# Prompt and sample step of an mLSTM–HGRN2 layer: another order of projection blocks, keys and queries in one tile, and weight sums that a transfer adds in place

## The chip, the cores and the metric

The kernel runs on one core of a Trainium2 chip. The metric is the device time of one execution in microseconds (us). Before the change the median of three runs is 1180.33 us (1180.24 to 1180.45).

The engines are named as in the profile: PE (matrix multiply, with its weight loads as PEld), DVE (vector), ACT (scalar), POOL (GpSimd), SP (which issues most transfers). Each engine works through its own list of instructions in order and waits at one instruction until the semaphores of that instruction are there; what stands behind it waits too.

## The reference

One step of a hybrid layer over 544 tokens: 512 of a new prompt and 32 of a running stream. All matrices are float32.

```python
xn = rmsnorm(x); proj = xn @ w_in                       # 1024 -> 12 blocks of columns
u, v, z, ig, fg, q_h, f_h, i_h, g_h, ga, gb = split(proj)
c  = silu(causal_conv(u))
hm = mlstm(c @ w_qm, c @ w_km, v, ig, lf, C, n, m)      # 4 heads of 512, chunks, matrix memory C
hm = (layernorm(hm) + m_skip * c) * silu(z);  ya = hm @ w_brm
f  = lb + (1 - lb) * sigmoid(f_h);  k = (1 - lb) * sigmoid(-f_h);  q = silu(q_h)
oh = hgrn(q, k, i_h, log f, S)                          # 8 heads of 128, gated linear attention
oh = head_rmsnorm(oh) * silu(g_h);               yb = oh @ w_brh
h  = x + (sigmoid(ga) * ya + sigmoid(gb) * yb) @ w_out
h  = h + sigmoid(h @ w_pg) * (p @ w_ple);        out = rmsnorm(h)
```

The new states (convolution rows, C, n, m, S) of both streams are outputs as well.

## The kernel before

**Numbers.** Every float32 product is made of three: an operand is split into a high part (ACT rounds it, L103 or L130) and the rest (DVE subtracts, L104 or L131), and PE multiplies high by high, high by low and low by high.

**Projections.** The product of `xn` with the columns of `w_in` goes by *units* of 128 output columns, two units a and b at a time (a *pair*, class `Two`). The inner dimension of 1024 is cut in half, so the weights of a pair are four pieces of 128x512: a11 and a12 (unit a, first and second half), a21 and a22 (unit b). A Strassen-like scheme makes seven products instead of eight, with a11, a12, a22 and the sums s1 = a21 + a22, s2 = s1 + a11, s3 = a11 + a21, s4 = s2 + a12. Each of the seven is a *block*: a 128x512 piece, cast by ACT and completed by DVE, then 4 x 3 matmuls of 272 columns into one of the pair's two PSUM halves (tile `d`). Between blocks ACT copies a partial result out (`keep`, L481, tile `t`), and DVE adds or subtracts a partial result into the destination (`put`, L488 and L490). a11, s2, s3 and a22 gather in the first half, a12, s1 and s4 in the second. The sums s1 and s3 of *early* pairs are not computed by DVE: SP loads one piece into a tile `ws` (L404) and POOL issues a second transfer that adds the other (L405). s2 and s4 are added by DVE (L430). So POOL holds such a transfer until the load of its base has landed.

**Order.** PE's list is written out by hand (`manual_schedule`); the lists of DVE, ACT, POOL and SP follow the program order and priorities through a scheduler. `Pump` holds all blocks of all pairs of a stage, sorted by times from a table (`HEAD` for a first pair, `NEXT` for the others: the blocks of one pair interleave with those of the next), and emits them in half steps of six matmuls. *Chains* (`mchain` for a head of the mLSTM, `chain` for a head of HGRN2) yield numbers; at each yield that many half steps of projection go onto PE's list, and the weights of up to `AHEAD` = 3 blocks more are prepared. Rings of buffers bind this: raw pieces `NRAW` = 8, high and low pieces `NPIECE` = 5 each, sums `NSUM` = 5, token-wide tiles `NSLOT` = 26.

**Stages.** After the norm come four mLSTM heads: projections run beside the chain of the head; at its end the head's result `hm` (four tiles, L1083 to L1085 and the split at L104) is multiplied by `w_brm` in `stage_br` (24 matmuls for each of eight results, tile `ya`, weights `wbm..`), and for heads after the first DVE adds the former sum (`y`, L1103). For the last head, 16 half steps of the HGRN2 projections are pumped ahead of `stage_br(3)`. Then the eight HGRN2 heads: for each, the pairs q/f and g/i, and `chain(h)`. It has seven levels c = 1, 2, 4, ..., 64: ACT packs keys into `km` (L1438), three half steps of projection follow, four matmuls give `pl` (L1446), DVE scales half of the keys and half of the queries (`hk`, `hq`, L1464, in four operations) and copies the level's part of `pl` under a mask into `at` (L1473). After the last level keys are transposed (`ht`, L1510), the output `ho` is formed, and ACT scales the head's output by the root-mean-square factor `hr` (L1564, four 128x128 pieces, and L1565). Then come eight pairs `ga` and `gb` (the merge), `p @ w_ple`, `yb`, `w_out` and `w_pg`.

The order of a pair's blocks, and what the pump does before the last `stage_br`:

```python
ALONE, HEAD, NEXT = (0, 1, 2, 3), (0, 3, 1, 6, 5, 9, 11), (0, 3, 5, 6, 8, 9, 11)   # a11 s2 a12 s3 s1 a22 s4
...
pump.to(8 * LASTBR)
stage_br(MH - 1)
```

## Time and profile before

| what | value |
|---|---|
| median of three runs | 1180.33 us |
| the profiled execution, its own time | 1178.68 us |
| its span in the trace | 1176.7 us |
| PE busy | 1140.0 us, 8897 records |
| DVE busy | 891.7 us (76%) |
| ACT busy | 708.9 us (60%) |
| POOL busy | 181.6 us (15%) |
| mean granted clock of PE | 0.997 |

The span lies 1.98 us below the execution's own time. Stages by the trace: head 0's `ya` runs at 179.1 to 203.6 us, the last head's `ya` at 619.0 to 651.3, the HGRN2 heads between about 650 and 950, the merge after that. A row of the windows view gives, for a stretch from A to B, its length, then busy time and count for PE, PEld, DVE, ACT and POOL, the granted clock of PE, the share of time that the transfer engines were busy, and GB/s. A row of the waits view gives the instruction that waited, the one that released it, the sum in us, how often, and the longest.

### The profile page before, as it was taken

The page shows a single profiled execution, that of the slowest core. Times are in us where ns is not written, and L with a number is a line of the kernel's source. Part 1 is how long each engine was busy: PE and PEld are TensorE (multiplying, and loading weights), DVE is VectorE, ACT ScalarE, POOL GpSimd, SP SyncE. Part 2 cuts the span into 40 slices and gives each one's busy share as a digit, 9 for nine tenths or more (in the row PEclk, how much of TensorE's full clock was granted, in tenths as well). Part 3 has the DMA queues.
Part 4 walks back from the last instruction along what each step waited for, and adds up shares of the span by engine and source line. Part 5 has one row for each costly group of instructions (what it writes and reads, how often), then busy time and mean ns, then how long its engine had stood idle before and what let it go on. Part 6 is the DMA issues. An engine that isn't in the chain of part 4 may idle for free. (4 is left out here: it accounts for less than half of the span.)

```text
span 1176.7 us, 24263 instructions
## 1 busy us (share of the span) xinstructions
PE 1140.0 (97%) x8897; PEld 1110.7 (94%) x8897; DVE 891.7 (76%) x2092; ACT 708.9 (60%) x1565; POOL 181.6 (15%) x335
## 2 busy tenths in 40 slices
PE   9999999999999999999988999999999989999998
PEld 9998999999999999999977999899989989999998
DVE  6977987686996768967883788898888767654485
ACT  5676567554765547565552577777777755433462
POOL 4942001110011001110100112221122210000000
PEclk9999999999999999999989999999999999999999
DMA  6233215232452324434836544544444585332653
GB/s 228 64 117 103 93 48 183 100 110 99 137 175 92 107 102 130 158 121 144 243 94 209 137 123 113 117 108 111 118 116 125 142 236 150 110 98 78 235 169 113
DMA packets 88270, 154.69 MB, mean 131 GB/s; under 512 B 9940, under 2 KB 17492, under 8 KB 88152
## 3 DMA queue, kind: packets, MB, share of 16 engines
q1 hardware_dynamic: 81072, 140.50, 36.5%
q0 software_dynamic: 6912, 12.59, 6.9%
q8 instruction: 70, 1.15, 0.4%
q14 instruction: 48, 0.39, 0.1%
q10 hardware_dynamic: 168, 0.06, 0.0%
HBM read 128.19 MB, written 24.91 MB: 130 GB/s over the span
## 5 line engine op out<-in xcount | busy, mean ns | idle before, releaser
L405 POOL DMA_DIRECT2D ws<-in_w_in x48 | 42.1, 877 | 301.8 <-DMA ws<-in_w_in 57.4
L481 ACT COPY t<-d 128x272 f32<-128x272 f32 x126 | 47.5, 377 | 2.7 <-PE d L467 2.2
L1446 PE MATMUL pl<-hq,km 128*128 128x128 f32 x224 | 37.1, 289 | 8.6 <-ACT km L1438 8.5
L601 DVE SCALAR_TENSOR_TENSOR cv<-ub,vec,cv 128x547 f32<-128x547 f32 x48 | 40.3, 841 | 2.9 <-ACT cv L596 2.1
L1446 PEld LDWEIGHTS pl<-hq,km 128*128 128x128 f32 x224 | 30.9, 190 | 11.0 <-ACT km L1438 10.8
L965 DVE SCALAR_TENSOR_TENSOR c<-c,wi,Cs 128x258 f32<-128x258 f32 x32 | 15.3, 478 | 21.6 <-PE Cs L963 21.5
L1438 ACT COPY km<-hk 128x256 f32<-128x256 f32 x56 | 23.5, 419 | 10.3 <-DVE rsq_u L168 5.8
L1103 DVE TENSOR_TENSOR y<-ya,y 128x272 f32<-128x272 f32 x48 | 18.8, 434 | 13.6 <-PE ya L151 13.4
L877 ACT COPY Co<-C 128x258 f32<-128x258 f32 x32 | 10.4, 378 | 28.9 <-PE C L865 22.1
L1473 DVE COPY_PREDICATED at<-lmask,pl 128x288 f32<-128x288 uint8 (+1 forms) x56 | 26.3, 469 | 0.0
L1464 DVE TENSOR_TENSOR hq<-hq,q 128x128 f32<-128x128 f32 (+1 forms) x96 | 25.2, 290 | 0.9
L1421 POOL TENSOR_SCALAR_AFFINE_SELECT aa<-at 128x128 f32<-128x128 f32 x32 | 25.5, 829 | 2.3 <-DVE at L1473 2.3
L1464 DVE TENSOR_TENSOR hk<-hk,q 128x144 f32<-128x144 f32 (+1 forms) x96 | 25.1, 290 | 0.7
L593 POOL COPY uo<-ub 128x3 f32<-128x3 f32 x16 | 17.5, 1092 | 39.0 <-DVE ub L490 28.8
L1046 ACT COPY y<-nm 128x516 f32<-128x516 f32 x16 | 9.4, 590 | 21.6 <-PE nm L1035 21.6
L763 POOL COPY vsm<-vt 128x96 f32<-128x96 f32 x16 | 6.0, 383 | 88.2 <-ACT vt L492 44.8
L865 PE MATMUL C<-vh,kwl 128*128 128x258 f32 x96 | 19.4, 283 | 0.0
L865 PE MATMUL C<-vh,kwh 128*128 128x258 f32 x96 | 19.4, 283 | 0.0
L865 PE MATMUL C<-vl,kwh 128*128 128x258 f32 x96 | 19.4, 283 | 0.0
L839 ACT CAST sh<-dm 128x512 fp32r<-128x512 f32 (+3 forms) x16 | 7.4, 460 | 19.6 <-DVE dm L833 18.1
L1559 ACT ACTIVATE osq<-kq 128x128 f32<-128x128 f32 x32 | 9.9, 310 | 15.1 <-DVE kq L1553 14.8
L995 DVE BATCH_NORM_STATS2 bs<-y 128x6 f32<-128x512 f32 (+1 forms) x20 | 13.8, 689 | 6.3 <-ACT y L1046 6.2
(4471 smaller groups left out, 5072.4 us busy)
## 6 DMA issues: line engine op xcount, KB each, us to landing
ws<-in_w_in SPq DMA_DIRECT2D x48, 256.0 KB, 3.4
ws<-in_w_in POOLq DMA_DIRECT2D x48, 256.0 KB, 4.4
ya_d<-y SPq DMA_DIRECT2D x32, 272.0 KB, 2.5
y<-ya_d SPq DMA_DIRECT2D x24, 272.0 KB, 3.4
c<-in_C SPq DMA_DIRECT2D x16, 258.0 KB, 3.8
out_Cp<-Co SPq DMA_DIRECT2D x16, 258.0 KB, 2.7
out_Cs<-c SPq DMA_DIRECT2D x16, 258.0 KB, 2.7
x<-in_xT SPq DMA_DIRECT2D x8, 272.5 KB, 4.7
```

The costliest lines, as they stand in the source:

```text
L405: G.dma_start(t, w_in[u][:, i * WP : (i + 1) * WP], accum_op=ALU.add)
L481: S.copy(t, ps)
L593: G.tensor_copy(uo[:, ft, 0, :], ub[:, 547:550])
L601: V.scalar_tensor_tensor(cv[:, :547], ub[:, j : j + 547], vcol(V_CW + 4 * ft + j), cv[:, :547], ALU.mult, ALU.add)
L865: PE.matmul(pn[g][:, :VH], kw[b][x][:, f * P : (f + 1) * P], vv[b][y][:, g * VH : (g + 1) * VH], start=(b == 0 and j == 0), stop=(b == NB ...
L965: V.scalar_tensor_tensor(c0[f][:, v], c0[f][:, v], wi[:, NS - 1 : NS], pn[:, :VH], ALU.mult, ALU.add)
L1103: V.tensor_tensor(y[:, half(b)], acc[b], y[:, half(b)], ALU.add)
L1421: G.affine_select(out=out, in_=x, compare_op=ALU.is_gt, fill=0.0, base=0, pattern=[[-sign, n]], channel_multiplier=sign)
L1438: S.copy(km.rearrange("p (n j c) -> p n j c", j=2, c=c), view(kk, HB, ((2 * c, NA // (2 * c)), (c - HB, 2), (1, c))),)
L1446: PE.matmul(pn[:, 0, b * P : (b + 1) * P], km[:, b * P : (b + 1) * P], view(qq, b * P, ((2 * c, P // (2 * c)), (HB + c, 2), (1, c))), star ...
L1464: V.tensor_tensor(xv[:, :, i, :], xv[:, :, i, :], t[:, :, 1 - i : 2 - i].to_broadcast([P, m, c]), ALU.mult)
L1473: V.copy_predicated(at[:, :n], lmask[:, li, :n], pn[:, 0, :n])
```

## The change

1. *Order of a pair.* One table `PAIR` serves every pair: a11, a12, then s2, s1, s3, with a22 and s4 of the former pair between a12 and s2. s1 and s2 are prepared together. A pair marked `apart` (head 0's q/f, no longer early) takes eleven places, so that it ends before the next begins. Before the last `stage_br` the pump runs to the end of that pair's q and prepares nothing of later pairs (`pump.limit`).
2. *Sums.* One tile is reused in place: s1, then s2, then s4 (`NSUM` 5 to 4). In early pairs the last addition (s2 to s4) is a transfer that POOL issues and that adds the piece in place, after s2 has been split.
3. *Keys and queries.* A head's keys and queries are the two halves of one tile of 2 x 550 (`hkq`), so that a level's scalings are two operations, each on a keys part and a queries part, in place of four. `NSLOT` falls to 22. Two of the four `vh`/`vl` pairs of an mLSTM head use the same new buffers.
4. *Priorities.* The `km` copy, the scalings, the masked copy, the transposed copies and the end of a head's chain are placed with high priority.
5. *Small moves.* `silu(z)` of the first head: two DVE copies out of PSUM, then one ACT operation (before, two ACT operations from PSUM). The `hr` scaling moves from ACT (five operations for a head) to DVE (two). `hv` is set by POOL instead of DVE. `finish(h - 1)` comes one level later. Before the memory products of the mLSTM the pump goes on to a point where fewer than two pairs are open (`clear`).

The matrix products are the same. Instructions in the program: DVE 2094 to 1977, ACT 1531 to 1487, POOL 340 to 369, SP 565 to 564.

```diff
-            return [(a, 0)] + ([] if self.early else [(b, 0)]) + [(b, 1), (a, 1)]
+            return [(a, 0), (a, 1)] + ([] if self.early else [(b, 0)]) + [(b, 1)]
...
+            s1 = [] if self.early else [(b, 0), (b, 1)]
             return [
                 (times[0], [(a, 0)], self.make("a11"), self.run("a11", 0, True, self.after1), []),
...
+                (times[1], [(a, 1)], self.make("a12"), self.run("a12", 1, True, self.after2), []),
+                (times[2], [], None, self.run("s1", 1, True, self.after5), []),
+                (times[3], s1, self.make("s1", "s2"), self.run("s2", 0, False, self.after6), []),
+                (times[4], [], self.make("s3"), self.run("s3", 0, False, self.after7), []),
+                (times[5], [(b, 1)] if self.early else [], self.make("a22"), self.run("a22", 0, False, self.after4), [k[1]]),
                 (times[6], [], self.make("s4"), self.run("s4", 1, False, self.after3), [k[0]]),
...
+            if form == "s2":
+                add(q["s1"], q["s1"], raw[a, 0])
...
+            if form == "s2" and self.early:
+                G.dma_start(q["s1"], w_in[a][:, WP : 2 * WP], accum_op=ALU.add)
+            elif form == "s2":
+                add(q["s1"], q["s1"], raw[a, 1])
...
-    ALONE, HEAD, NEXT = (0, 1, 2, 3), (0, 3, 1, 6, 5, 9, 11), (0, 3, 5, 6, 8, 9, 11)
+    ALONE, PAIR = (0, 1, 2, 3), (0, 1, 5, 4, 6, 9, 10)
...
+                    times, length = PAIR, 11 if e.apart else 7
...
+        def clear(self, n):
+            while True:
+                i = (self.done + n) // 2
+                begun = {x for x, _ in self.ids[:i]} & {x for x, _ in self.ids[i:]}
+                if (self.done + n) % 2 == 0 and len(begun) < 2:
+                    return n
+                n += 1
...
-                act = S.activation(z[:, b * TH : (b + 1) * TH], acc[b][:, :TH], AF.Silu)
+                with tc.high_priority():
+                    V.tensor_copy(z[:, b * TH : (b + 1) * TH], acc[b][:, :TH])
+            act = S.activation(z[:, :T], z[:, :T], AF.Silu)
...
-        yield 4
+        yield pump.clear(4)
...
-            for x, far in ((kk, True), (qq, False)):
...
-                    V.tensor_tensor(
-                        xv[:, :, i, :], xv[:, :, i, :], t[:, :, 1 - i : 2 - i].to_broadcast([P, m, c]), ALU.mult
+            with tc.high_priority():
...
+                    x = view(
+                        kk, lo + first * c, ((qoff + (1 - 2 * first) * c, 2), (2 * c, m), (1, c))
                     )
...
+                    V.tensor_tensor(x, x, d, ALU.mult)
...
-        for b in range(NB):
-            S.mul(ov[:, b * P : (b + 1) * P], ov[:, b * P : (b + 1) * P], hr[:, b : b + 1])
-        S.mul(osb, osb, hr[:NS, NB : NB + 1])
+        V.tensor_tensor(
+            ov[:, :NP].rearrange("p (b e) -> p b e", b=NB),
...
-        pump.to(8 * LASTBR)
+
+        pump.limit = pump.when["q", 0] // 2
+        pump.to(pump.when["q", 0])
         stage_br(MH - 1)
+        pump.limit = None
```

How the order moves is shown at three places.

**PE, ahead of the last `stage_br`.** Each row is the first matmul of a block (pair 48 is head 0's q/f, pair 72 its g/i; `ws148` is that pair's s1, `wa1172` a piece of the next). Before:

```order
L467 MATMUL d_8645<-xfh_1561,ws248h 128x272 [waits Activation_49]
L467 MATMUL d_8646<-xfh_1561,ws148h 128x272 [waits DVE_49]
L467 MATMUL d_8645<-xfh_1561,ws348h 128x272 [waits Activation_49]
L467 MATMUL d_8749<-xh_510,wa1172h 128x272
L467 MATMUL d_8645<-xfh_1561,wa2248h 128x272 [waits Activation_49]
L467 MATMUL d_8749<-xfh_1561,ws272h 128x272 [waits Activation_49]
L151 MATMUL ya_8827<-hm12h,wbm300h 128x272 [waits Activation_49]
```

Changed:

```order
L476 MATMUL d_8614<-xfh_1562,ws248h 128x272 [waits Activation_49]
L476 MATMUL d_8615<-xfh_1562,ws148h 128x272
L476 MATMUL d_8614<-xfh_1562,ws348h 128x272 [waits Activation_49]
L476 MATMUL d_8614<-xfh_1562,wa2248h 128x272 [waits Activation_49]
L476 MATMUL d_8615<-xh_603,ws448h 128x272 [waits DVE_49]
L151 MATMUL ya_8758<-hm12h,wbm300h 128x272
```

All seven blocks of pair 48 now stand ahead of `ya`, and none of pair 72.

**DVE, at the same place.** `hq` (before) and `hkq` (changed) is the `put` that frees the second PSUM half for s1; `hm12l` to `hm15l` are the rests of the head's result. Before:

```order
L104 TENSOR_TENSOR hm14l<-c_7041,hm14h 128x544 [waits DMAHW5_49,Activation_49]
L1085 TENSOR_TENSOR c_7129<-c_7129,z_8148 128x544 [waits DVE_49]
L131 TENSOR_TENSOR wa1172l<-wi72r_8612,wa1172h 128x512 [waits DMAHW1_49]
L131 TENSOR_TENSOR wa2248l<-wi56r_8610,wa2248h 128x512 [waits DMAHW0_49,PE_49]
L104 TENSOR_TENSOR hm15l<-c_7129,hm15h 128x544 [waits DMAHW0_49,Activation_49,Pool_49]
L488 TENSOR_TENSOR hq_8647<-d_8646,t_8661 128x272
```

Changed:

```order
L1106 SCALAR_TENSOR_TENSOR c_6773<-yt_8518,vec,c_6773 128x512 [waits PE_49]
L1107 SCALAR_TENSOR_TENSOR c_6773<-yt_8518,vec,c_6773 128x32
L1106 SCALAR_TENSOR_TENSOR c_6937<-yt_8532,vec,c_6937 128x512 [waits PE_49]
L1108 TENSOR_TENSOR c_6773<-c_6773,z_7961 128x544 [waits DVE_49]
L497 TENSOR_TENSOR hkq_8616<-d_8615,t_8630 128x272 [waits DMAHW2_49,DMAHW3_49,PE_49,Activation_49]
L1107 SCALAR_TENSOR_TENSOR c_6937<-yt_8532,vec,c_6937 128x32
```

The `put` stood behind the last split of the head's result; now it stands behind two of the four additions that come ahead of the first split.

**DVE, one level of an HGRN2 head.** Level c = 4 of the head whose tiles are `hk_10409` before and `hkq_10029` after. Before:

```order
L1464 TENSOR_TENSOR hk_10409<-hk_10409,q_10465 128x36x4 [waits PE_49]
L168 SCALAR_TENSOR_TENSOR rsq_u<-rsq_u,hv 128x5 [waits DVE_49]
L1464 TENSOR_TENSOR hk_10409<-hk_10409,q_10465 128x32x4
L169 SCALAR_TENSOR_TENSOR hr<-rsq_u,hr 128x5 [waits DVE_49]
L1464 TENSOR_TENSOR hq_10075<-hq_10075,q_10465 128x36x4
L1464 TENSOR_TENSOR hq_10075<-hq_10075,q_10465 128x32x4
L1473 COPY_PREDICATED at_10681<-lmask,pl_10808 128x288
```

Changed:

```order
L1501 TENSOR_TENSOR hkq_10029<-hkq_10029,q_10371 128x2x36x4 [waits PE_49]
L1508 COPY_PREDICATED at_10610<-lmask,pl_10733 128x288
L1501 TENSOR_TENSOR hkq_10029<-hkq_10029,q_10371 128x2x32x4 [waits DVE_49]
L169 SCALAR_TENSOR_TENSOR hr<-rsq_u,hr 128x5
L439 TENSOR_TENSOR ws_10517<-ws_10517,wi76r_10234 128x512
```

Four scalings are two, and the masked copy stands between them; the next `km` copy (on ACT) needs both.

152 lines of the change are left out of this document (83 added, 69 removed).

## Prediction

> **What bounds the kernel now.** I first read the busy times of the engines, then windows by stage.
>
> ```profile
> PE 1140.0 (97%) x8897; PEld 1110.7 (94%) x8897; DVE 891.7 (76%) x2092; ACT 708.9 (60%) x1565; POOL 181.6 (15%) x335
> ```
> ```profile
> core 0: us, PE busy (x) PEld busy (x) DVE busy (x) ACT busy (x) POOL busy (x), PEclk, DMA share, GB/s
> 602.70:608.40 5.70, 0.46 (x4) 0.24 (x2) 5.62 (x11) 1.73 (x4) 0.00 (x0) 0.88 0.00 1
> 608.40:614.00 5.60, 5.54 (x24) 5.54 (x25) 2.67 (x5) 1.24 (x2) 0.87 (x1) 0.51 0.60 165
> 650.00:950.00 300.00, 288.55 (x2261) 276.58 (x2260) 254.76 (x768) 219.73 (x547) 60.69 (x82) 1.00 0.50 123
> 125.00:600.00 475.00, 473.98 (x3736) 466.16 (x3736) 376.40 (x805) 284.64 (x598) 52.91 (x142) 1.00 0.40 129
> 950.00:1000.00 50.00, 46.02 (x361) 45.32 (x361) 34.62 (x61) 29.14 (x60) 5.21 (x6) 1.00 0.68 193
> 1025.00:1050.00 25.00, 25.00 (x202) 25.00 (x201) 13.73 (x26) 7.53 (x13) 0.00 (x0) 1.00 0.27 86
> 100.00:125.00 25.00, 23.68 (x181) 22.41 (x180) 24.58 (x52) 15.18 (x31) 4.38 (x12) 1.00 0.18 56
> ```
>
> PE sets the time. From 125 to 600 us it is busy for 473.98 of 475: nothing is to be had there. What can be had lies in four places: the step from the mLSTM to HGRN2 (602 to 651), the HGRN2 heads (11.45 us of 300 not busy), the merge (3.98 of 50), and the start. At full pace 202 matmuls take 25 us, 0.124 each. The change moves no matmul out of the program, so it can win only PE's waits and half-clock time. Those are, by the view of what PE waited for (sum, times, longest):
>
> ```profile
> PE pl L1446 <- ACT km L1438: 8.5, 9, 1.1
> PE d L467 <- DVE hq L488: 5.3, 1, 5.3
> PE d L467 <- ACT t L481: 3.0, 2, 2.1
> PE ht L1510 <- DVE hq L1464: 2.6, 6, 0.4
> PE k L151 <- ACT z L635: 2.2, 1, 2.2
> PE ya L151 <- DVE y L1103: 1.6, 4, 0.4
> PE ya L151 <- ACT wbm301h L130: 1.2, 1, 1.2
> PE d L467 <- DVE gb L488: 1.0, 1, 1.0
> PE Cs L963 <- DVE c L965: 1.0, 3, 0.5
> ```
>
> **A, the step to HGRN2.** One wait of 5.3 us stands out. On DVE's timeline its releaser comes last:
>
> ```profile
> 607.34 0.72 DVE L104 TENSOR_TENSOR hm15l<-c,hm15h 128x544 fp32r<-128x544 f32 x1
> 607.97 0.43 DVE L488 TENSOR_TENSOR hq<-d,t 128x272 f32<-128x272 f32 x1
> ```
>
> DVE is busy 5.62 of the 5.70 us, on the end of the head's result; the `put` of 0.43 us that frees a PSUM half is last in that queue. In the changed order it stands behind two additions of the four, ahead of every split, and before the block that needs it PE has another block of 12 matmuls (1.5 us) and two groups of transposes. I take the 5.3 us as gone. Behind that wait 24 matmuls took 5.54 us at a granted clock of 0.51; at 0.124 they take 3.0, so 2.5 us more go with it. [...]
>
> Then `stage_br`, by the rows of tile `ya` alone, the first head's and the last head's:
>
> ```profile
> 179.10:203.60 24.50, 24.18 (x192) 23.96 (x192) 0.00 (x0) 4.99 (x16) 1.00 0.60 199
> 619.00:651.30 32.30, 27.91 (x192) 24.93 (x192) 5.52 (x14) 0.00 (x0) 1.00 0.60 188
> ```
>
> The same 192 matmuls took 24.2 us when no projection pair was open beside them, and 32.3 for the last head. There three pieces of open pairs (`ws448`, `wa1272`, `ws372`) hold three of five weight buffers and the pairs hold four PSUM halves, so `ya` has two halves, and each result waits for the addition two matmuls ahead. In the changed order nothing is open. 32.3 − 24.2 = 8.1, to which I add 0.3 for the trailing casts: A is −(5.3 + 2.5 + 8.1 + 0.3) = −16.2. New waits: a22 of the pair comes right behind s3, so it stands behind a copy out of PSUM that may follow a cast on ACT (0.38 and 0.62 by the rows under F and E), with the handing over some 1.2 us; and the first `wbm` rest on DVE may be 0.5 to 1.7 late. I take +2.5, with 0 and +8 as ends (+8: the `put` late again by most of its 5.3 us, with the half clock). A: −13.7.
>
> **B, the start.** `k` waits 2.2 us for `silu(z)` on ACT. Two DVE copies (0.43 each by the like-sized `hq` row above) now free PSUM. But DVE is busy 24.58 of 25 us there, and eight copies add 3.4 us to it; I take −2.2 + 0.5 = −1.7 (ends −2.2 and +1.2, all of the 3.4 on the path).
>
> **C, the HGRN2 heads.** The 8.5 us ahead of `pl` come nearly all from one level of each head:
>
> ```profile
> 738.86 1.28 ACT L1564 ACTIVATE kq<-kq,hr 128x128 f32<-128x128 f32 x4
> 740.04 0.39 ACT L1565 ACTIVATE osb<-osb,hr 32x128 f32<-32x128 f32 x1
> 740.34 0.39 ACT L1438 COPY km<-hk 128x256 f32<-128x256 f32 x1
> 740.78 0.71 PE L1446 MATMUL pl<-hq,km 128*128 128x128 f32 x4 [1.13 <-ACT km L1438]
> ```
>
> The `hr` scaling of the former head, 1.67 us on ACT, stands ahead of `km`. It goes to DVE as one 128x512 operation and a small one, and `km` gets priority: the wait loses its cause seven times over, 7 x 1.13 = 7.9 of the 8.5. What could take its place is the scaling that `km` needs:
>
> ```profile
> L1464 DVE TENSOR_TENSOR hk<-hk,q 128x128 f32<-128x128 f32 x64 | 17.0, 284 | 0.0
> L1464 DVE TENSOR_TENSOR hk<-hk,q 128x144 f32<-128x144 f32 x32 | 9.7, 304 | 0.7
> L488 DVE TENSOR_TENSOR hg<-d,t 128x272 f32<-128x272 f32 x16 | 6.9, 431 | 0.3 <-PE d L467 0.3
> L1553 DVE TENSOR_TENSOR kq<-ho,kq 128x512 f32<-128x512 f32 x8 | 5.5, 692 | 4.4 <-PE ho L1552 4.4
> L1473 DVE COPY_PREDICATED at<-lmask,pl 128x288 f32<-128x288 uint8 x40 | 19.2, 479 | 0.0
> L1438 ACT COPY km<-hk 128x256 f32<-128x256 f32 x55 | 22.9, 417 | 10.3 <-DVE rsq_u L168 5.8 <-DVE hk L1464 4.5
> ```
>
> From 128 to 272 elements a row grows by 147 ns, about one per element; 256 and 288 elements make 0.42 and 0.45 us. `km` needed two of four operations before (0.28 + 0.30) and needs both now (0.87), and the masked copy may stand between (0.48 at most). With `km` that is 0.87 + 0.42 = 1.29, or 1.8 with the masked copy; between a level's `pl` and the next one lie three half steps, 18 matmuls or 2.25 us. It fits by 0.4 to 0.9. One place is tighter: where a sigmoid's work stands ahead of `km` on ACT, I allow 0.3 in seven heads, +2. The wait of `ht` for the last scaling (2.6) shrinks, since 0.87 replaces 4 x 0.29 = 1.16: −1.2. The 15.6 us that ACT sheds in this stage are not on the path. C is −7.9 − 1.2 + 2 = −7.1; ends −11.1 (both rows gone) and 0.
>
> DVE sheds work here too: 56 levels x 0.29 = 16 and 21 additions of 0.69 = 14.5, against some 8 for `hr`. It was 85% busy, so that helps every `put`.
>
> **D, the mLSTM's memory products.** `Cs` waited 1.0 us in all for its addition; `clear` leaves it a PSUM half more: −1.0.
>
> **E, the merge.** A cast on ACT waits for a late load, and a copy out of PSUM behind it holds PE:
>
> ```profile
> 958.28 0.64 ACT L103 CAST ps0h<-p 128x544 fp32r<-128x544 f32 x1 [4.16 <-DMA p<-in_pT]
> 959.81 0.39 PE L467 MATMUL d<-xfh,ws384h 128*128 128x272 f32 x1 [2.07 <-ACT t L481]
> ```
>
> With 3.0 for `t` and 1.0 for `gb`, 4.0 is the most to be won; raw pieces now come free after their own split (the adding transfer reads the weights anew), so SP's queue, in which that load stands, moves sooner. Against it comes the new chain of one sum tile: split of s2, POOL's issue, transfer, split of s4, base of the next sum, its adding transfer, split.
>
> ```profile
> ws<-in_w_in POOLq DMA_DIRECT2D x7, 256.0 KB, 4.8
> ws<-in_w_in SPq DMA_DIRECT2D x6, 256.0 KB, 4.4
> L405 POOL DMA_DIRECT2D ws<-in_w_in x48 | 42.1, 877 | 301.8 <-DMA ws<-in_w_in 57.4
> L130 ACT CAST ws384h<-ws x1: 622/622/622, 951.7 to 951.7; 128x512 fp32r<-128x512 f32 x1
> L131 DVE TENSOR_TENSOR ws384l<-ws,ws384h x1: 680/680/680, 954.0 to 954.0; 128x512 fp32r<-128x512 f32 x1
> ```
>
> POOL's queue is one: behind a waiting adding transfer stand the next pair's sums. A turn of it costs 4.4 (base) + 0.87 + 4.8 + 1.3 (split) = 11.4 us, and seven blocks of 12 matmuls pass in 84 x 0.124 = 10.4. So in the merge it may drift by 1.0 a pair once about 4 us of lead are used, some +2.5 over the last pairs. In the HGRN2 heads sixteen pairs share the 300 us, over 17 each, and there it hides. E is −4.0 + 2.5 = −1.5 (ends −4.0 and, as a rival, far above). [...]
>
> **F, the closer blocks.**
>
> ```profile
> L481 ACT COPY t<-d 128x272 f32<-128x272 f32 x126 | 47.5, 377 | 2.7 <-PE d L467 2.2
> ```
>
> s3 now follows s2's copy out of PSUM with one block between, 1.5 us, where two lay before. The copy takes 0.38 and can stand behind one cast of 0.62; a longer queue costs. Two of the 126 copies made PE wait before, 3.0 us together (the waits above); I take +1 (ends 0 and +3).
>
> **Sum.** −13.7 − 1.7 − 7.1 − 1.0 − 1.5 + 1.0 = −24.0. The profiled execution took 1178.68 us, its span 1176.7; the median of the runs is 1.65 above the former. 1178.68 − 24.0 + 1.65 = 1156.3; I say 1156. The lowest that the rows allow: all of the listed waits (26.4), the half clock (2.5), and what of `ya` the list doesn't hold (8.1 − 2.8 = 5.3), 34 in all, 1146. With the upper ends of A, B and F the forecast's own range reaches 1156 + 5.5 + 2.9 + 2 = 1166; its likely part is 1148 to 1163.
>
> **Rivals.**
>
> *R1, POOL's queue turns into the bound (slower).* The third transfer of each pair enters one queue, in order. It decides from the point where a turn lasts more than PE's 10.4 us from the first merge pair on, not only as drift: with two transfers at 5.7, the largest landing time in the merge, a turn is 5.7 + 0.87 + 5.7 + 1.3 = 13.6, +3.2 a pair; where the adding transfer waits for one base load more (4.4) each of eight pairs loses 7.6, 61 less the 4 of lead. Between them, about half of the way, +32 on 1156 gives 1188. For it: POOL already waits 301.8 us at its sums, 57.4 of it for their bases; the transfer engines' share is highest there, 0.68. Against: the median turn is 11.4.
>
> *R2, the scalings come late at every level.* If another DVE operation of 0.69 and a cast of 0.62 regularly stand ahead, the 0.4 to 0.9 of room is gone and each level waits 0.1 to 0.5 us: 56 x 0.15 = 8 gives 1164, 56 x 0.5 = 28 gives 1184. For it: DVE at 85%. Against: priority, and less work on DVE.
>
> *R3, the change does not do what it says in A.* The `put` still ends behind DVE's queue: +5.3 and 2.5 at half clock, 1164. For it: it still has two additions ahead of it that wait for PE's transposes. Against: the order above.
>
> **How the numbers follow.** Forecast 0.65, R1 0.13, R2 0.11, R3 0.11. R3 and half of R2 are still faster: 0.65 + 0.11 + 0.06 = 0.82. A difference within 0.2% (about 2.4 us) is what a measurement of this kernel can't tell from none; R2 passes through it, 0.04. Slower: R1 and the rest of R2, 0.14. The range 1146 to 1172 holds the forecast, R3 and the lower half of R2, 0.82.
>
> **What would show it.** A: no wait over 3 us at about 600 us, clock 1.00 there, the last 192 `ya` matmuls within 26 us. C: the HGRN2 heads' PE with under 5 us of waits in 300, the combined scaling at 0.42 to 0.45 us, none of PE's waits at `pl` near 1.1. E and R1: PE's waits in the merge, and POOL's idle time ahead of its adding transfers and what ended it. I am wrong if PE waits for casts of `ws4` pieces pair after pair (R1), for `km` at most levels (R2), or if the time of 125 to 600 us, where PE had 1.0 us to spare, grows by more than 3.

## The result, and the profile after

The changed kernel takes 1184.37 us (median of seven runs, 1181.96 to 1186.9), the kernel before 1180.24 us over the same seven rounds. The ratio is 1.0039 with an interval of 1.0027 to 1.0052: slower by about 4 us, where 24 us less were forecast.

The page of the profile after: PE's share is unchanged, the instructions fell as planned, and a row for the adding transfers is new.

```profile
PE 1146.8 (97%) x8897; PEld 1117.9 (95%) x8897; DVE 885.4 (75%) x1975; ACT 701.1 (59%) x1521; POOL 186.7 (16%) x364
...
L451 POOL DMA_DIRECT2D ws<-in_w_in x23 | 23.7, 1031 | 60.6 <-DVE ws272l L131 26.1
```

What PE waited for, after:

```profile
PE d L476 <- ACT t L490: 9.5, 6, 3.5
PE pl L1479 <- ACT km L1471: 4.4, 8, 1.5
PE k L151 <- DVE z L653: 4.1, 1, 4.1
PE d L476 <- DVE ws348l L131: 1.8, 1, 1.8
PE vt L951 <- DVE vhl L959: 1.4, 2, 0.9
...
PE ht L1546 <- ACT kit L1550: 1.1, 6, 0.2
...
PE d L476 <- DVE ws26l L131: 0.9, 1, 0.9
...
```

The 5.3 us of the late `put` are gone, the waits of `ya` for its additions fell from 1.6 to 0.3, and those at `pl` and `ht` are about halved. But `t` rose from 3.0 to 9.5, `k` from 2.2 to 4.1, and the rests of s2 and s3 on DVE are new (`ws348l`, and 0.9 us each at `ws26l`, `ws210l` and `ws214l`, the s2 of the last pair of three mLSTM stages). The windows of the changed kernel by stage (the columns are those of the windows shown before; each row begins with its stretch and its length):

```profile
70.30:167.10 96.80, 90.22 (x696) 87.94 (x696) 76.25 (x195) 59.59 (x126) 18.44 (x47) 0.96 0.28 93
167.10:186.90 19.80, 17.64 (x131) 16.14 (x130) 17.93 (x34) 10.56 (x22) 1.76 (x6) 1.00 0.27 76
186.90:339.20 152.30, 150.14 (x1188) 147.85 (x1187) 113.73 (x242) 93.51 (x200) 13.13 (x46) 1.00 0.38 122
339.20:492.10 152.90, 150.72 (x1189) 148.23 (x1188) 116.83 (x239) 89.22 (x184) 13.50 (x46) 1.00 0.37 120
492.10:627.30 135.20, 131.39 (x1008) 128.50 (x1007) 106.54 (x220) 82.57 (x167) 13.55 (x32) 0.97 0.47 147
627.30:652.30 25.00, 24.56 (x195) 24.14 (x194) 14.53 (x35) 8.56 (x16) 0.00 (x0) 1.00 0.84 272
652.30:929.80 277.50, 271.77 (x2107) 259.59 (x2106) 233.19 (x604) 196.42 (x474) 70.66 (x104) 1.00 0.61 139
929.80:1009.90 80.10, 73.01 (x541) 71.34 (x539) 49.96 (x98) 45.87 (x100) 11.45 (x14) 0.94 0.72 178
```

The end of stage 0 in the kernel before, for comparison with the second row:

```profile
162.00:179.10 17.10, 17.04 (x130) 15.98 (x128) 15.33 (x30) 10.22 (x22) 3.07 (x6) 1.00 0.11 32
```

All stages beside those of the kernel before:

| stage, from and to which matmuls | before, us | after, us | difference | at equal work |
|---|---|---|---|---|
| first `k` of head 0 to its transposes `yt` | 92.0 | 96.8 | +4.8 | +4.8 |
| `yt` to the first `ya` (end of stage 0) | 17.1 | 19.8 | +2.7 | +2.7 |
| `ya` of head 0 to `ya` of head 1 | 150.5 | 152.3 | +1.8 | +1.8 |
| `ya` of head 1 to `ya` of head 2 | 150.5 | 152.9 | +2.4 | +2.4 |
| `ya` of head 2 to `ya` of head 3 | 139.0 | 135.2 | −3.8 | −2.3 |
| `ya` of head 3 | 32.3 | 25.0 | −7.3 | −7.3 |
| to the `ho` of the last HGRN2 head | 277.4 | 277.5 | +0.1 | −2.8 |
| merge, to the first `yb` | 75.1 | 80.1 | +5.0 | +6.5 |

The last column allows for matmuls that the order moves over a boundary, at 0.124 us each: 12 fewer ahead of the last `ya`, 23 more by the records in the HGRN2 heads, 12 fewer in the merge. The sum is +5.8; the span grew by 1182.7 − 1176.7 = 6.0 between the two profiled executions, the medians by 4.1.

### The profile page after: what moved, and what is told of

It is laid out like the page before. It is cut to its first block, busy times and chain, and to the rows that moved or that the text cites. A ratio compares the mean times of both kernels' runs of the same rounds, so it can differ in the third digit from the quotient of the medians.

```text
span 1182.7 us, 24120 instructions
## 1 busy us (share of the span) xinstructions
PE 1146.8 (97%) x8897; PEld 1117.9 (95%) x8897; DVE 885.4 (75%) x1975; ACT 701.1 (59%) x1521; POOL 186.7 (16%) x364
## 4 chain that ended last, share of the span: by engine, by line
PE 80%; DVE 9%; ACT 5%; DMA 4%; issue 3%; SPq 0%; POOL 0%; ACTq 0%; DVEq 0%; POOLq 0%
PE d L476 31%; PE ya L151 8%; PE pg L1691 4%; PE yb L151 4%; PE o L151 4%; PE k L151 4%; PE q L151 4%; PE C L884 4%; PE pl L1479 2%; PE nm L1058 2%; PE sc L844 2%; DMA ws<-in_w_in 2%; PE d L369 1%; DVE cv L618 1%; PE ple L151 1%
## 5 line engine op out<-in xcount | busy, mean ns | idle before, releaser
L405 POOL DMA_DIRECT2D ws<-in_w_in x46 | 40.4, 877 | 163.5 <-DMA ws<-in_w_in 36.8
L1501 DVE TENSOR_TENSOR hkq<-hkq,q 128x288 f32<-128x288 f32 (+1 forms) x96 | 40.8, 432 | 16.3 <-PE pl L1479 12.6
L1479 PE MATMUL pl<-hkq,km 128*128 128x128 f32 x224 | 39.4, 298 | 4.5 <-ACT km L1471 4.4
L1479 PEld LDWEIGHTS pl<-hkq,km 128*128 128x128 f32 x224 | 30.9, 189 | 7.7 <-ACT km L1471 6.4
L1471 ACT COPY km<-hkq 128x256 f32<-128x256 f32 x56 | 23.9, 427 | 16.2 <-PE d L476 12.3
L451 POOL DMA_DIRECT2D ws<-in_w_in x23 | 23.7, 1031 | 60.6 <-DVE ws272l L131 26.1
L1452 POOL TENSOR_SCALAR_AFFINE_SELECT aa<-at 128x128 f32<-128x128 f32 x32 | 20.7, 678 | 43.1 <-DVE at L1508 38.4
L1058 PE MATMUL nm<-vhl,sh 128*128 128x258 f32 x112 | 18.3, 286 | 0.0
L960 POOL CAST vhl<-one 128x4 fp32r<-128x4 f32 x8 | 2.7, 340 | 98.1 <-PE nm L1058 98.1
L1678 DVE TENSOR_TENSOR h<-o,h 128x272 f32<-128x272 f32 x16 | 6.3, 437 | 14.5 <-PE o L151 14.5
L1665 DVE TENSOR_TENSOR gb<-yb,gb 128x272 f32<-128x272 f32 x16 | 6.3, 437 | 14.4 <-PE yb L151 14.4
```

What stands on the lines that cost most here:

```text
L405: G.dma_start(t, w_in[u][:, i * WP : (i + 1) * WP], accum_op=ALU.add)
L1058: PE.matmul(pn[:, g, :VH], st[j][x][:, (i - j) * P : (i - j + 1) * P], vv[j][y][:, g * VH : (g + 1) * VH], start=(j == 0 and q == 0), stop ...
L1471: S.copy(km.rearrange("p (n j c) -> p n j c", j=2, c=c), view(kk, HB, ((2 * c, NA // (2 * c)), (c - HB, 2), (1, c))),)
L1479: PE.matmul(pn[:, 0, b * P : (b + 1) * P], km[:, b * P : (b + 1) * P], view(qq, b * P, ((2 * c, P // (2 * c)), (HB + c, 2), (1, c))), star ...
L1501: V.tensor_tensor(x, x, d, ALU.mult)
```

## The experiments

The changed kernel's runs spread over 5 us, so where a difference is below 3 us the text reads the trace. One place differs from profile to profile though the edits lie elsewhere. From `ya` of head 0 to `ya` of head 1 it takes 152.3 us in the changed kernel, and 153.9 to 156.2 in the profiles of five runs below (DVE's last sum, p's casts, the last pair's order, silu(z) on ACT, the masked copy). In those five DVE stands 1.6 to 2.3 us at a sum s1 whose weights land late, and the rests of v (`vhl`), for which PE's transposes wait, stand behind it; in the changed kernel's own profile DVE stands there for 0.26 us. From the run with DVE's last sum:

```profile
273.79 0.69 DVE L439 TENSOR_TENSOR ws<-wi9r,wi9r 128x512 f32<-128x512 f32 x1 [1.94 <-DMA wi9r<-in_w_in]
274.40 0.68 DVE L957 TENSOR_TENSOR vhl<-vt,vhl 128x512 fp32r<-128x512 f32 x1
...
275.13 0.44 PE L949 MATMUL vt<-ident,vt 128*128 128x128 f32 x2 [2.02 <-DVE vhl L957]
```

So up to 4 us of a total can come from this place. Which part of the change brings the load so near its limit was not tried.

**DVE's last sum.** The adding transfer undone:

```diff
-            if form == "s2" and self.early:
-                G.dma_start(q["s1"], w_in[a][:, WP : 2 * WP], accum_op=ALU.add)
-            elif form == "s2":
+            if form == "s2":
                 add(q["s1"], q["s1"], raw[a, 1])
```

> The changed kernel, but in early pairs DVE adds the last piece (s2 to s4) as in the other pairs, and POOL issues no third transfer. Theory: only the second long wait of the merge, at 999 us (2.6 us and some 14 matmuls at half clock), comes from the adding transfer, so the time falls by 3 to 4.5 us. Rival R1 (POOL's queue bounds the merge): both long waits of the merge go, 6 to 9 us. Rival (DVE's 23 additions of 0.69 us cost more than they save): no change or up to 3 us slower.

1176.84 us, ratio to before 0.9975 (0.9963 to 0.9988): 7.5 less than the changed kernel. In the merge one wait of 1.7 us is left of two (3.5 and 2.5). That is the size that R1 was given here (6 to 9 us), not mine (3 to 4.5).

**The casts of p placed later.**

```diff
...
-        ps_.append(split(t[:, :T], f"ps{k}"))
+        with tc.issue_after(merged[5].ins):
+            ps_.append(split(t[:, :T], f"ps{k}"))
```

> The changed kernel, but the casts of the two p tiles on ACT are placed behind the sigmoid of the sixth ga unit, some 25 us later, when p has landed. Theory (the first long wait of the merge, 3.5 us at 962 us with 25 matmuls at half clock behind it, comes from ACT standing 3.4 us at the cast of p): the time falls by 5 to 6.5 us. Rival R1 (ACT would then stand at the casts of sums that the transfers bring late): the wait moves to a cast of a sum, 0 to 1.5 us.

1184.42 us, 1.0035 (1.0022 to 1.0049): nothing won, and the wait moved to a cast of a sum, as expected under R1. The profiled execution of this run took 1190.44 us, 6.0 more than the median, so its trace shows where the wait went and not what it cost in the median. The changed kernel's timeline at both waits, in the merge:

```profile
958.24 0.65 ACT L103 CAST ps0h<-p 128x544 fp32r<-128x544 f32 x1 [3.42 <-DMA p<-in_pT]
...
962.30 0.60 PE L476 MATMUL d<-xfh,ws384h 128*128 128x272 f32 x1 [3.45 <-ACT t L490]
...
997.79 0.62 ACT L130 CAST ws494h<-ws 128x512 fp32r<-128x512 f32 x1 [3.19 <-DMA ws<-in_w_in]
...
999.30 0.60 PE L476 MATMUL d<-xfh,ws394h 128*128 128x272 f32 x1 [2.48 <-ACT t L490]
```

And the timeline of this run, with the casts of p out of the way:

```profile
969.94 0.62 ACT L130 CAST ws484h<-ws 128x512 fp32r<-128x512 f32 x1 [7.13 <-DMA ws<-in_w_in]
...
971.42 0.59 PE L476 MATMUL d<-xfh,wa2284h 128*128 128x272 f32 x1 [3.38 <-ACT t L490]
```

The brackets tell it: ACT idles for a transfer, then PE for the copy `t` that stands behind that cast on ACT. With p's cast moved, ACT stands 7.13 us at the cast of s4, which waits for the adding transfer, and PE waits 3.38 us instead of 3.45. In this execution the wait at p had only hidden the other.

**The sums as before.** s1 and s2 in tiles of their own, s1 split at its own block, last sum by DVE:

```diff
-                (times[2], [], None, self.run("s1", 1, True, self.after5), []),
-                (times[3], s1, self.make("s1", "s2"),
+                (times[2], [], self.make("s1"), self.run("s1", 1, True, self.after5), []),
+                (times[3], s1, self.make("s2"),
...
```

> The changed kernel with all of the sums as before the change: s1 and s2 in tiles of their own (NSUM 5), s1 split at its own block, the last sum by DVE. Theory (the adding transfer costs some 7.5 us in the merge, as the run with DVE's last sum showed, and the one tile in place puts the split of s1 ahead of the sum s2, so that the rest of s2 comes 0.9 to 1.1 us late at the end of each mLSTM stage): 9 to 11 us less than the changed kernel, 1173 to 1175, and the three waits for the rest of s2 gone. Rival (the shared tile costs nothing, the waits at the end of a stage come from DVE's load alone): as with DVE's last sum only, 1177, the three waits still there.

1175.31 us, 0.9963 (0.9948 to 0.9978). The merge now waits 0.5 us at `t`. At the ends of the mLSTM stages the waits for the rest of s2 are gone, and three of 0.9 to 1.3 us for the rest of s1 stand in their place (`PE d L474 <- DVE ws110l L131` is one); ahead of the last `ya` the wait for `ws348l` is 2.9 us instead of 1.8. So in this order the shared tile only decides which rest is late. The median lies at the theory's edge and its interval meets that of the run before: of the 9 us, some 7.5 are the adding transfer, and whether the shared tile costs anything is not decided.

**Another order for the last pair of a stage.** a11, s2, a12, s3, s1, a22, s4 for a stage's last pair:

```diff
+    LAST = (0, 5, 8, 4, 6, 9, 10)
-                    times, length = PAIR, 11 if e.apart else 7
+                    times, length = LAST if n + 1 == len(todo) and not e.early else PAIR, 11 if e.apart else 7
```

> The changed kernel, but the last pair of each mLSTM stage goes a11, s2, a12, s3, s1, a22, s4, so that a block lies between s2 and s3 and between s3 and a22. Theory (with no next pair the new table puts a22 right behind s3, and PE waits for the copy out of PSUM, 1.08 us at three places, and for the rest of s2, 1.1 us at three places): the three waits at a22 go, those at s2 stay or go, the time falls by 3 to 6 us. Rival (DVE is full at the end of a stage, 21 to 23 of 25 us, so the waits only move to s2): 0 to 1 us.

1186.48 us, 1.0048 (1.0032 to 1.0064). The waits at a22 are gone; waits of the same size at the rest of s3 and at the transposes `yt` (3.1 us in three) took their place, and 3.6 us at the rest of s2 ahead of the last `ya`. The rival was right that the waits only move. Its reason fits the windows (DVE is busy 17.93 of 19.80 us at the end of stage 0), but was not tried by itself. The total is 2 us above the changed kernel's, within what the place named at the head of this section can make (155.7 us there in this profile).

**Order and sums as before.** The edit of "The sums as before" and, besides, the tables `HEAD` and `NEXT` again; the rest of the change is kept. The second part of the edit:

```diff
...
-    ALONE, PAIR = (0, 1, 2, 3), (0, 1, 5, 4, 6, 9, 10)
+    ALONE, HEAD, NEXT = (0, 1, 2, 3), (0, 1, 5, 3, 6, 9, 11), (0, 5, 8, 3, 6, 9, 11)
...
```

> The changed kernel with the sums as before the change and also the order of blocks as before (tables HEAD and NEXT); the shared tile of keys and queries, the two scalings, the pair that stands apart, the priorities and the small moves stay. Theory (the order puts a22 right behind s3 in the last pair of each mLSTM stage, and in the HGRN2 heads it puts the end of f's block just ahead of a level, so that km waits on ACT behind the flip of f): the six waits of 1.0 to 1.4 us at the ends of the stages and the 0.58 us per head go, 1163 to 1168 us, 8 to 12 less than with the sums alone undone. Rival (these waits belong to the shared tile, the two scalings or DVE's load): 1172 to 1176.

1166.29 us, 0.9887 (0.9872 to 0.9902): 9.0 less than with the sums alone undone. All six waits at the stage ends are gone, and of the waits at `pl` 0.9 us in two are left. By the traces the stretch from `yt` of head 0 to the last `ya` is 8.5 us shorter than in the run with the sums alone undone, so it is the order that makes the ends of the stages dear. Two waits are left or new: 1.8 us for the rest of a22 (`wa2248l`) ahead of the last `ya`, and 2.1 us in seven at `hoT`, which waits for the scaled output on DVE; a head takes 33.2 us. The order of before with the shared sum tile was not run, so whether separate sums are needed as well stays open.

**silu(z) from PSUM on ACT.** The two copies undone:

```diff
-                with tc.high_priority():
-                    V.tensor_copy(z[:, b * TH : (b + 1) * TH], acc[b][:, :TH])
-            act = S.activation(z[:, :T], z[:, :T], AF.Silu)
+                act = S.activation(z[:, b * TH : (b + 1) * TH], acc[b][:, :TH], AF.Silu)
```

> The changed kernel with the first head's silu(z) straight from PSUM on ACT again, as before the change. Theory (each new wait stands by itself, and one of them is the copy of z on DVE behind a scan of 2.23 us): PE's wait for k falls from 4.1 us to about 2.2, and the half clock behind it (11 matmuls between 77.5 and 80 us) goes, so the time falls by 3 to 4.5 us against the changed kernel. Rival (what made the kernel slower lies in the merge, in POOL's queue of sums): at most 0.5 us.

1182.88 us, 1.0023 (1.0006 to 1.0039), an interval that meets the changed kernel's, so the time alone decides nothing. The trace does: `k` waits 2.2 us instead of 4.1, and from the first `k` to `yt` it takes 93.7 us instead of 96.8, 3.1 less, with 92.0 in the kernel before. In that profile, of an execution of 1187.97 us, other places took longer, `ya` of head 0 to `ya` of head 1 among them (156.2 us). The changed kernel's timeline at this place:

```profile
74.10 2.23 DVE L698 TENSOR_TENSOR_SCAN row<-rst,row 4x544 f32<-4x544 f32 x1
76.37 0.77 DVE L699 SCALAR_TENSOR_TENSOR row<-ig,vec,row 4x544 f32<-4x544 f32 x1
77.07 0.77 DVE L653 COPY z<-d 128x272 f32<-128x272 f32 x2
...
77.55 0.94 PE L151 MATMUL k<-cs0h,wk000h 128*128 128x272 f32 x2 [4.12 <-DVE z L653]
```

The copies that free PSUM stand behind a scan of 2.23 us and an operation of 0.77. In the kernel before, ACT loaded a table there (1.28 us) and then read PSUM itself (0.69 us for both halves), and `k` waited 2.2 us.

**Priority for the splits of the pair that stands apart.**

```diff
-            self.w[form] = split_piece(src, f"w{form}{a}")
+            with tc.high_priority() if self.apart else nullcontext():
+                self.w[form] = split_piece(src, f"w{form}{a}")
```

> The changed kernel, but the weight splits of the pair ahead of the last stage_br (head 0's q/f) have high priority. Theory (PE's wait of 1.8 us for the rest of s3, behind four operations of the head's result on DVE, and some 30 matmuls at half clock behind it are what the step to HGRN2 still loses): 4 to 5 us less than the changed kernel, the wait for the copy ahead of a22 (1.1 us) still there. Rival (DVE then brings the head's result late and PE waits at the first ya instead): 0 to 1 us less.

1179.1 us, 0.9993 (0.998 to 1.0005): 5.3 less than the changed kernel, a little more than the theory's 4 to 5. From 600 to 650 us PE's clock is 1.00; the wait for `ws348l` is gone, the one at `t` is 0.5 us (0.8 before the edit), and `ya` waits 1.1 us for its additions (0.3 before the edit). The changed kernel's timeline there shows what went:

```profile
618.53 0.68 DVE L131 TENSOR_TENSOR ws348l<-ws,ws348h 128x512 fp32r<-128x512 f32 x1
...
619.26 0.40 PE L476 MATMUL d<-xfh,ws348l 128*128 128x272 f32 x1 [1.82 <-DVE ws348l L131]
```

**One part on the kernel before: the pair apart.**

```diff
...
-                True,
+                h > 0,
+                h == 0,
...
-        pump.to(8 * LASTBR)
+        pump.limit = pump.when["q", 0] // 2
+        pump.to(pump.when["q", 0])
         stage_br(MH - 1)
+        pump.limit = None
```

> The kernel before with one part of the change: head 0's q/f pair stands apart, not early, and ends ahead of the last stage_br, with nothing of later pairs prepared. Theory (an open pair costs stage_br its 8 us; the put of that pair still stands behind the last split on DVE here, so the long wait stays): 6 to 9 us less than before, the last 192 ya matmuls in 24.5 us, a wait of 4 to 6 us and a half clock still ahead of s1. Rival, the prediction's reading (the long wait goes with the order of blocks): 12 to 15 us less than before.

1173.75 us, 0.9951 (0.9938 to 0.9964), 6.4 less. The last `ya` takes 24.1 us, and `PE d L467 <- DVE hq L488: 5.3, 1, 5.3` stands as before. So an open pair costs `stage_br` its 8 us, and the late `put` is another matter.

**One part on the kernel before: the `hr` scaling on DVE, priority for `km`.**

```diff
+            with tc.high_priority():
...
-        for b in range(NB):
-            S.mul(ov[:, b * P : (b + 1) * P], ov[:, b * P : (b + 1) * P], hr[:, b : b + 1])
-        S.mul(osb, osb, hr[:NS, NB : NB + 1])
+        V.tensor_tensor(
+            ov[:, :NP].rearrange("p (b e) -> p b e", b=NB),
+            ov[:, :NP].rearrange("p (b e) -> p b e", b=NB),
+            hr[:, :NB].rearrange("p (b o) -> p b o", o=1).to_broadcast([P, NB, P]),
+            ALU.mult,
+        )
+        V.tensor_scalar(osb, osb, hr[:NS, NB : NB + 1], None, ALU.mult)
```

> The kernel before with one part of the change: the hr scaling on DVE (two operations for a head), the km copy with high priority, the four scalings as they were. Theory (the wait of 1.13 us per head goes, and nothing takes its place while km needs two short scalings only): 6 to 8 us less than before. Rival (in ACT's list km then stands behind the flip of f, which waits for its block on PE, whatever the scalings are, so each head waits 0.6 to 0.8 us at another level): 2 to 4 us less.

1170.65 us, 0.9931 (0.9913 to 0.9949), 9.5 less, more than the 6 to 8 expected. In the HGRN2 heads this is all that PE waits for, once a head; `pl` has none (a wait of 1.7 us at `gb` comes in the merge):

```profile
PE ht L1511 <- ACT kit L1514: 3.3, 7, 1.1
```

From one head's first `ho` to the next it takes 32.5 us, against 34.0 before and 33.5 in the changed kernel.

**Both parts on the kernel before.** The two diffs above together.

> The kernel before with two parts of the change: head 0's q/f pair apart, and the hr scaling on DVE with priority for km. Theory (the two gains lie in different stages and add): 6.4 and 9.5 us less than before, 1163 to 1166 us. Rival (part of each gain was the state of one transfer queue in the merge, which both need): 1167 to 1171.

1164.32 us, 0.9872 (0.9856 to 0.9888). The gains add: 15.7 us of 6.4 + 9.5.

**Four scalings in the changed kernel.** The keys and queries stay in one tile:

```diff
-                for t, lo, m, first, _ in sides:
-                    x = view(
-                        kk, lo + first * c, ((qoff + (1 - 2 * first) * c, 2), (2 * c, m), (1, c))
-                    )
-                    d = bass.AP(
-                        t.tensor, t.offset + 1 - first, [list(t.ap[0]), [2 * first - 1, 2], [2, m], [0, c]]
-                    )
-                    V.tensor_tensor(x, x, d, ALU.mult)
+                for x, far in ((kk, True), (qq, False)):
+                    for t, lo, m, first, _ in sides:
+                        i = first if far else 1 - first
+                        xv = x[:, lo : lo + 2 * c * m].rearrange("p (n t c) -> p n t c", t=2, c=c)
+                        tv = t.rearrange("p (n t) -> p n t", t=2)
+                        V.tensor_tensor(
+                            xv[:, :, i, :], xv[:, :, i, :], tv[:, :, 1 - i : 2 - i].to_broadcast([P, m, c]), ALU.mult
+                        )
```

> The changed kernel with four scalings a level again (the keys and queries still in one tile). Theory (km waits behind the flip of f on ACT, not for the scalings): no change within 1.5 us, PE's 0.58 us per head ahead of pl still there. Rival R2 (km now needs two operations of 0.41 and 0.45 us, and that makes it late): the 0.58 us goes, 3 to 5 us less than the changed kernel.

1174.87 us, 0.9958 (0.9946 to 0.9971): 9.5 us less than the changed kernel. The rival R2 was right and my theory wrong: `pl` waits no more, and a head takes 32.5 us again. The size is above R2's 3 to 5 as well: 8.3 us lie between the last `ya` and the last head's `ho`, 1.0 a head, where only the 0.58 of the wait itself had been counted. The timeline of the changed kernel and then of this one, at the same level (`wa1152h` is the same cast, `kq<-d` the flip of f):

```profile
746.03 0.62 ACT L130 CAST wa1152h<-wi52r 128x512 fp32r<-128x512 f32 x1 [0.81 <-PE d L476]
...
746.55 0.39 ACT L501 ACTIVATE kq<-d 128x272 f32<-128x272 f32 x1
...
746.84 0.40 ACT L1471 COPY km<-hkq 128x256 f32<-128x256 f32 x1
...
747.29 0.72 PE L1479 MATMUL pl<-hkq,km 128*128 128x128 f32 x4 [0.42 <-ACT km L1471]
```
```profile
743.45 0.41 ACT L1471 COPY km<-hkq 128x256 f32<-128x256 f32 x1 [0.40 <-DVE hkq L1498]
743.95 0.62 ACT L130 CAST wa1152h<-wi52r 128x512 fp32r<-128x512 f32 x1
744.48 0.39 ACT L501 ACTIVATE kq<-d 128x272 f32<-128x272 f32 x1
```

With two scalings `km` stands on ACT behind the cast and the flip, and ACT waits for PE at the cast; with four it stands ahead of both. So I had the right neighbour on ACT and the wrong reason for its place: what puts `km` behind it are the two scalings, by this run; how they do it is the next question.

**The masked copy behind both scalings.**

```diff
-                    V.tensor_tensor(x, x, d, ALU.mult)
+                    scaled = V.tensor_tensor(x, x, d, ALU.mult)
...
+            with tc.high_priority(), tc.issue_after(scaled.ins):
                 V.copy_predicated(at[:, :n], lmask[:, li, :n], pn[:, 0, :n])
```

> The changed kernel with the two scalings a level, but the masked copy always behind the second of them. Theory (what the two operations lose against four is the masked copy of 0.48 us that stands between them and so ahead of km): the time between the heads falls from 33.5 to 32.4 to 32.8 us, 5 to 9 us less than the changed kernel. Rival (the second long operation waits for the first, and km needs both, whatever stands between): the head stays above 33.1 us, 0 to 3 us less.

1187.21 us, 1.0064 (1.0046 to 1.0083); a head takes 33.8 us. The time is above both expectations (it was to fall), 2.8 us over the changed kernel. The head's time is the rival's: not the masked copy, for DVE's list in this run has something else between the two.

```profile
743.40 0.45 DVE L1501 TENSOR_TENSOR hkq<-hkq,q 128x288 f32<-128x288 f32 x1
743.77 0.16 DVE L169 SCALAR_TENSOR_TENSOR hr<-rsq_u,hr 128x5 f32<-128x5 f32 x1
743.85 0.68 DVE L439 TENSOR_TENSOR ws<-ws,wi75r 128x512 f32<-128x512 f32 x1
744.45 0.42 DVE L1501 TENSOR_TENSOR hkq<-hkq,q 128x256 f32<-128x256 f32 x1
```

At the level shown ahead of the prediction, the second of the two scalings carries a wait on DVE's own semaphore, which none of the last three of the four does. My reading is that the scheduler fills that place, and `km` needs the second. That this wait is the cause was not tried by itself.

**The best combination: order and sums of before, silu(z) on ACT, splits with priority.** It keeps the pair apart, the `hr` scaling on DVE, the shared tile and the priorities.

> As the run with order and sums of before, and besides silu(z) on ACT from PSUM, and high priority for the splits of the pair that stands apart. Theory (each of the two is worth what its own run or trace showed, 3.2 us at the start and 4 to 5 us at the step to HGRN2): 1154 to 1160 us, faster than both kernels. Rival (with DVE freed at the step the wait goes elsewhere, as it partly did with the changed kernel): 1161 to 1165.

1161.08 us, 0.9839 (0.9821 to 0.9856), 18.9 us less than before and the fastest of all. It reached the rival's figure: the two edits give 5.2 us together where 7 to 8 were expected. A wait of 1.4 us at `gb` is new against the run with order and sums of before; 1.7 us at `hoT` stay from it.

**The same with four scalings.**

> The best run so far (order and sums of before, silu(z) on ACT, splits of the pair that stands apart with priority) with four scalings a level. Theory (the two operations cost each head 0.7 us there too, 33.2 against 32.5 between heads): 1154 to 1157 us. Rival (in the order of before the two operations were not late, so the 33.2 has another cause): 1160 to 1162.

1173.62 us, 0.9952 (0.9935 to 0.997), 12.5 us slower. Neither expectation: the waits at `pl` go, this row comes, and a head takes 34.4 us or more, where it took 33.2.

```profile
PE hoT L1612 <- DVE kq L1598: 14.1, 7, 3.5
```

With four scalings in that order, the `hr` scaling on DVE comes so late that `finish` waits for it, about 2 us a head. Whether two or four operations are better is a matter of the list that they end up in.

## Why the prediction was wrong, point by point

**The step to HGRN2 (A: −13.7, measured −9.6).** Right in its parts: the last `ya` takes 25.0 us where 24.2 was taken, and the `put` holds nothing up. The new waits, 1.8 and 0.8 us, were foreseen as 2.5. What failed is that the sum counts every new wait at its own length and no half clock behind it. That was the author's estimate, and no run shows it: behind four waits of 1.82 to 4.12 us the changed kernel's trace has a clock of 0.50 to 0.58. The windows of the changed kernel around its four long waits, each time first the wait, then what follows:

```profile
75.00:78.00 3.00, 0.45 (x2) 0.39 (x2) 2.96 (x8) 0.26 (x2) 0.19 (x1) 0.86 0.30 89
78.00:81.00 3.00, 3.00 (x16) 3.00 (x16) 2.93 (x10) 2.87 (x6) 0.52 (x1) 0.58 0.00 0
617.40:619.80 2.40, 0.58 (x5) 0.54 (x5) 2.40 (x5) 0.96 (x2) 0.00 (x0) 1.00 0.00 0
619.80:626.60 6.80, 5.99 (x27) 5.67 (x27) 4.90 (x9) 4.38 (x9) 1.74 (x2) 0.50 0.70 171
957.50:962.30 4.80, 1.35 (x12) 1.13 (x10) 2.77 (x5) 4.02 (x9) 2.65 (x3) 0.88 0.98 189
962.30:967.80 5.50, 5.50 (x24) 5.50 (x25) 3.44 (x6) 2.02 (x4) 0.00 (x0) 0.50 0.96 232
996.50:999.30 2.80, 0.32 (x4) 0.10 (x2) 0.85 (x2) 1.50 (x4) 0.00 (x0) 0.90 0.48 132
999.30:1002.00 2.70, 2.70 (x12) 2.70 (x13) 1.15 (x3) 0.55 (x2) 0.00 (x0) 0.50 0.32 93
```

After a wait of 1.82 us the clock stood at 0.50 for 6.8 us. At 0.124 us, 27 matmuls take 3.35 and the second wait 0.8, so half clock cost some 2.6 us here; by the same sum 2.5 at 962, 1.2 at 999 and 1.0 at 78. That is 7.3 us in four places against 2.5 in one before. Of the 4.1 us by which A missed, 2.6 are the half clock and 1.1 `ya`, which gave 7.3 where 8.4 was counted. With the splits given priority the step from `ya` of head 2 to the end of the last `ya` is 14.5 us shorter than before at equal work: the forecast's size.

**The start (B: −1.7, measured +4.8).** The failing step is the price of the copies. DVE's load was read in the window from 100 to 125 us, but the wait lay at 75, where DVE does a scan of 2.23 us and ACT is idle. The wait rose by 2 us, with half clock behind it, 3.1 us in all by the run with `silu(z)` on ACT, where −1.7 was forecast and +1.2 was the upper end. The other 1.7 of the +4.8 lie behind the first `q` (from there to `yt` 70.2 us, 68.5 before); no run isolates them.

**The HGRN2 heads (C: −7.1, measured −2.8).** The term for the `hr` scaling, with the priority for `km`, was right and even small: on the kernel before the two gave 1.5 us a head. The step that failed is the room of 0.4 to 0.9 us for `km`. It counted DVE's operations against PE's 18 matmuls and took ACT as free but for a sigmoid (the +2), but ACT works through a list, in which `km` had moved behind a cast that waits for PE. R2 named such a cast, for every level and at 0.15 to 0.5 us each; measured, it is one level of a head, and the two scalings cost 1.0 us a head.

**The mLSTM stages (D and F: together 0, measured +6.9).** The failing step is F's +1, which counted the copy between s2 and s3 alone. That a22 has the next pair's a11 and a12 between itself and s3 holds while a next pair follows. The last pair of a stage has none, so a22 stands right behind s3, and the rest of s2 comes late:

```profile
178.29 0.39 PE L476 MATMUL d<-xfh,ws26l 128*128 128x272 f32 x1 [0.94 <-DVE ws26l L131]
...
183.74 0.39 PE L476 MATMUL d<-xfh,wa226h 128*128 128x272 f32 x1 [0.91 <-ACT t L490]
```

At 0.125 us from one matmul to the next, each of these waits costs about 1.1 us, and a third of 0.3 us, for the cast of s2, stands ahead of them. Three stages times 2.5 make 7.5, near the 6.9 of the table. That it is the order that makes them is shown by the run with `HEAD` and `NEXT`, where they are gone. I had priced this very neighbourhood for the pair that stands apart (1.2 us under A) and not for the stages.

**The merge (E: −1.5, measured +6.5).** R1 named the right part, the third transfer, with 0.13 and a price of +32; undoing it gave 7.5. (R1's two ends are 8 x 3.2 − 4 = 22 and 61 − 4 = 57, so half of the way would have been 39.) Its mechanism, POOL's queue turning slower than PE pair after pair, is not what the traces show. For pair 84 the queue did hold a transfer up: the rest of s2 was ready at 955.0 us and the adding transfer was issued at 958.1, behind a sum whose base landed late. For the last pair it was free: POOL had idled 9.8 us and issued the transfer 0.4 us after the split, and the 4.0 us to its landing alone made ACT stand 3.19 us. The sum's step "it may drift by 1.0 a pair once some 4 us of lead are used, +2.5" was too small: two waits and the half clock behind them came to more. The transfers in the merge (from 940 to 1000 us):

```profile
ws<-in_w_in POOLq DMA_DIRECT2D x12, 256.0 KB, 5.4
ws<-in_w_in SPq DMA_DIRECT2D x6, 256.0 KB, 4.1
```

5.4 us took the place of the 4.8 in the sum: a turn is 4.1 + 0.88 + 5.4 + 1.3 = 11.7 us, not 11.4. The twelve are transfers of both kinds; the five adding ones alone landed in 6.2 us (4.0 to 7.3). Also missing was how a late sum reaches PE: not by its own block, but by ACT, where its cast stands ahead of the copy out of PSUM that PE waits for, as the prediction had described it for p alone.

**Sum.** −9.6 + 4.8 − 2.8 + 6.9 + 6.5 = +5.8. Two parts were worth about what the rows said, 15.7 us together on the kernel before. The other parts brought waits that the forecast priced at 0.5 to 2.5 us each, and the half clock behind them at nothing.

## What to carry to other kernels

A reordering has ends: check the distance between a producer and its consumer at the last element of each sequence, not in the steady state alone. Where an instruction moves to another engine, read that engine's list at the microsecond where the wait lies, and ask what the instruction will stand behind; an idle share, or the window next to it, says nothing. Parts of a change that the profile prices well are best taken alone: here two of them gave 1.3%, and the whole lost 0.4%.

## What the runs showed of the hardware

A wait of 1.82 us (at 619 us, after) was followed by a clock of 0.50, while one of 2.07 us (at 959.8, before) was not: the windows of the latter (957.5 to 959.8 us) and behind it (959.8 to 963.3) both show 1.00. The same wait went both ways: `k` waits 2.16 us for `silu(z)` on ACT in the kernel before, and 2.15 us in the run with the pair apart, whose code is the same there. In the former 25 matmuls follow in 3.4 us at a clock of 1.00 (75.3 to 78.7 us), in the latter 15 at 0.60 (75.6 to 79.0), and from `k` to `yt` it takes 93.5 us instead of 92.0. So the length of a wait did not decide alone in these traces: one of 1.82 to 2.48 us cost 1.2 to 2.6 us more, or nothing. What else decides is not shown by any run here.

In these traces short DVE operations that followed each other overlapped. In the run with four scalings:

```profile
742.84 0.92 DVE L1498 TENSOR_TENSOR hkq<-hkq,q 128x144 f32<-128x144 f32 x4
```

Four of 128 and 144 elements, listed at 285 and 302 ns each, take 0.92 us from the first's start to the last's end, not 1.17. Two of 256 and 288, listed at 0.42 and 0.46, overlapped as well; where they stand together in the changed kernel they take 0.79, not 0.88:

```profile
672.20 0.79 DVE L1501 TENSOR_TENSOR hkq<-hkq,q 128x288 f32<-128x288 f32 x2
```

So joining four in two saved 0.13 us here, where 0.29 was counted.
